# An encoder layer with two mixers: the weave of projection and convolution set to 400:329 instead of 445:329, and eight instead of five steps of the recurrence yielded beside the memory projection

## The chip, the cores and the metric

The kernel runs on one core of a Trainium2 chip. The core has a matrix engine (PE, TensorE), three engines for elementwise work (DVE or VectorE, ACT or ScalarE, POOL or GpSimd), and a queue engine (SP, SyncE) that mostly issues transfers. The metric is the device time of one execution in microseconds; the time of a kernel is the median of its runs.

## The reference, cut to what matters

One layer over 2048 rows of 1024 columns, all in fp32. One projection feeds two mixers: a long convolution (the Hyena half) and a bidirectional recurrence (the mLSTM half). Then come cross-attention into 256 memory rows and an MLP.

```python
u = _rms_norm(h, norm_mix_g[l])
proj = u @ w_in[l]
hy = _short_conv_centred(proj[..., :HY_COLS], hy_conv_w[l], hy_conv_b[l])
y_hy = _group_rms_norm(_hyena(hy, spec, hy_skip[l]), hy_norm_g[l], HYENA_GROUPS)
y_ml = _mlstm_bidirectional(q, k, v, o_pre, gates, ml_gate_b[l])
y_ml = _group_rms_norm(y_ml, ml_norm_g[l], MLSTM_HEADS)
h = h + concat(y_hy, y_ml) @ w_out[l]
h = h + _cross_attention(_rms_norm(h, norm_x_g[l]), _rms_norm(mem, norm_mem_g[l]), wq, wk, wv, wo)
h = h + square(relu(_rms_norm(h, norm_ff_g[l]) @ ff_w1[l])) @ ff_w2[l]
return _rms_norm(h, final_norm_g)
```

The Hyena half applies two filters, one after the other, each by transforms; they are called the first and the second order below. The mLSTM half runs one scan in each direction.

## The kernel before

Each fp32 gemm is split into a high and a low part and done as three products (helper `mm3`: lines 355, 358 and 359). Work is written as generators. Each `yield` carries an estimate of its length, and `weave(a, b, wa, wb)` advances `a` while what it has done, divided by `wa`, is not ahead of what `b` has done, divided by `wb`. So the weights are the lengths in which the two are meant to end together. What is written in this order is then ordered once more, before the run, by a scheduler that simulates the engines; it decides the final order on each engine, and each engine takes its instructions strictly in that order.

The stages that matter here, in the order of the source:

- **Projection and convolution.** `rest` is the projection: `sweep` (transposed columns) and `natural` (rows), with the gates of the recurrence (`gates`) and the states of its backward scan (`states`, fifteen of them, written to `cbd`) at its end. It is woven with `hyena`, the convolution. For each of the two orders the convolution does eight forward transforms (`spectrum`, L173/L186, input `f`; stored to `zs` by POOL's queue), sixteen block steps (L956 for the filter's response, L1030 and L987, loading `zs` and storing `zg`), and eight inverse transforms (L173/L186, input `e`). The first block step of an order needs all eight of its forward transforms.
- **The memory projection.** `memproj` yields eight heads of work: L708 (keys or values from memory), L725 and L737 (folded with the query and output weights). Its weights come through SP's queue (L415).
- **The recurrence.** `mlstm` takes sixteen steps of 128 rows, called chunks here. Chunk n issues the scores of chunk n+1 (L1284), for each direction sixteen products (L1322 within the chunk, L1324 with the state), and the update of the forward state (L1200, then L1206 on DVE). Its row factors are spread by DVE (L1275), masked and scaled by POOL (L1290, L1291), raised by ACT (L1293), multiplied with the scores by DVE (L1294). After every odd chunk the two newest chunks are normalised: squares on ACT (L1349), an inverse square root of thirteen small DVE operations (L211 to L216), then eight scalings (L1356). All products of a chunk go to a ring of four PSUM banks called `hy`, which the convolution and the transposes use too. The first `next` of the generator only loads and issues the scores of chunk 0, so n advances write n-1 chunks.
- **The attention.** It begins with transposes of the mixers' output (L1479) and with w_out, loaded at L1405 and split on ACT and DVE at L366. The remaining chunks are woven into it, and the MLP follows.

`beside_each(n, take(m, 5))` yields one advance of the memory projection and one of the recurrence in turn, with what is left of the five after that.

Of the kernel before, what the change touches and what calls it, by code (L numbers as in the profile page):

```python
# [2076 lines left out]
def chain(*gens):  # L2077
    for g in gens:
        yield from g


def weave(a, b, wa, wb, until=False):
    da = db = 0.0
    fa = fb = False
    while not (fa and fb):
        if fb or (not fa and da / wa <= db / wb):
            try:
                da += next(a)
            except StopIteration:
                fa = True  # L2090
        else:
            try:
                db += next(b)
            except StopIteration:
                fb = True
                if until:
                    return


def program(p):  # L2100
    with ExitStack() as ms:
        with ExitStack() as es:
            p.inproj_open(es)
            p.filters_open()
            p.prepq = p.x_first()
            p.pop()
            s = chain(p.sweep(range(4), 0, True, lambda: p.prep_x(1)), p.opened(), p.sweep(range(4), 1, False))
            f = p.filters()
            for _ in range(5):
                next(s)  # L2110
            next(f)
            next(f)
            next(s)
            weave(s, f, 140, 102, True)
            p.gates_open(es)
            n = p.memproj()
            m = p.mlstm(ms)
            with ExitStack() as hs:
                rest = chain(s, p.sweep(range(4, 10), 1, True), p.natural(1, (3, 0, 1, 2), True),
                             p.natural(0, (3,)), among(p.sweep((4, 5, 8, 9), 0, False), p.gates(), 2),  # L2120
                             among(chain(p.natural(0, (0, 1)), p.sweep((6, 7), 0, False),
                                         p.natural(0, (2,), p.prep_mem, 2)), p.states(), 1),
                             )
                weave(rest, p.hyena(hs), 445, 329)
            for _ in chain(p.turned_in(), take(n, 1), beside_each(n, take(m, 5))):
                pass
        with ExitStack() as rs:
            p.ts = rs.enter_context(ExitStack())
            p.tail_open(p.ts)
            with ExitStack() as at:  # L2130
                g = p.attention(at)
                weave(g, m, 440, 112, True)
                ms.close()
                p.ffn_open(rs)
                for _ in g:
                    pass
            p.ffn()


def among(g, h, every):  # L2140
    for i, v in enumerate(g):
        yield v
        if i % every == every - 1:
            next(h, None)
    for _ in h:
        pass


def beside_each(g, h):
    for v in g:  # L2150
        yield v
        yield next(h, 0)
    yield from h


def take(g, n):
    for _ in range(n):
        v = next(g, None)
        if v is None:
            return  # L2160
        yield v
# [31 lines left out]
```

## Time and profile before

| | us |
|---|---|
| median of 3 runs | 3072.69 |
| lowest and highest run | 3072.32, 3078.89 |
| profiled execution, its own time | 3076.22 |
| span of the profiled execution | 3074.5 |
| PE busy in the span | 2984.5 |
| convolution's last inverse transform (PE) | 1101 |
| chunk 0's scores (PE) | 1115 |
| memory projection's last product ends | 1122 |
| attention's first gemm product | 1179 |

The table's last four rows are times from the start of the span, read from the timeline of PE. In a row of the timeline the first two numbers are the start and the length in microseconds, then come the engine, the source line, the operation, what it writes and reads, its shape, how many instructions were merged, and in square brackets the idle time of that engine before it with what ended it. A matmul's length overlaps with the next one's start, so the pace of PE is read from start to start. Queue rows (SPq, or DMA_DIRECT2D on POOL) show when a transfer is issued.

### The profile page before, as it was taken

The numbers are of one execution on the slowest core, as the hardware profiler recorded it, in microseconds if no ns is written. First come the engines' busy times: TensorE is split into PE (matmuls) and PEld (weight loads), VectorE is DVE, ScalarE is ACT, GpSimd is POOL, SyncE is SP. The second block draws the span as 40 slices with busy tenths as digits, with TensorE's granted clock in tenths as the row PEclk, the third lists the DMA queues.
The fourth block names the chain that finished last, engine by engine and source line by source line (L and its number), as shares of the span: only waits on it lengthen the run. The fifth ranks groups of instructions, "written<-read, shape, count | busy, mean of one in ns | idle before, by whom it ended". The sixth has DMA issues, their size and how long they took to land.

```text
span 3074.5 us, 44129 instructions
## 1 busy us (share of the span) xinstructions
PE 2984.5 (97%) x14799; PEld 2369.8 (77%) x14799; DVE 1938.8 (63%) x3442; ACT 1493.0 (49%) x2930; POOL 1259.7 (41%) x1025
## 2 busy tenths in 40 slices
PE   9999999998999988999999999999999999999998
PEld 7666667775678757888887888888888888888876
DVE  7855454657656347867665665557555676566695
ACT  6443455635654236555544455556555543333335
POOL 0112123411344654333133247765566374344653
PEclk9999999999999988999999999999999999999999
DMA  6655687596877965464567466657544565344434
GB/s 219 196 188 171 214 271 219 184 297 200 258 223 249 349 231 192 158 220 131 188 203 259 147 210 216 208 181 243 186 154 151 195 198 171 118 158 120 155 103 164
DMA packets 423643, 607.03 MB, mean 197 GB/s; under 512 B 36846, under 2 KB 229998, under 8 KB 422392
## 3 DMA queue, kind: packets, MB, share of 16 engines
q1 hardware_dynamic: 395972, 525.42, 53.3%
q0 software_dynamic: 18992, 62.96, 5.6%
q10 hardware_dynamic: 8452, 15.83, 1.4%
q8 instruction: 117, 1.92, 0.3%
q14 instruction: 110, 0.90, 0.1%
HBM read 401.67 MB, written 202.41 MB: 196 GB/s over the span
## 4 chain that ended last, share of the span: by engine, by line
PE 58%; DVE 2%; DMA 1%; issue 1%; ACT 0%; POOL 0%; SPq 0%; DVEq 0%; ACTq 0%; POOLq 0%
PE mm L355 12%; PE mm L359 12%; PE mm L358 12%; PE hy L355 6%; PE hy L359 6%; PE hy L358 6%; PE hy L1322 1%; PE hy L1324 1%; DVE bl L1693 0%; PE hy L1284 0%; PE hy L1479 0%; PE hy L1596 0%; DVE acc L1991 0%; PE hy L1200 0%; DVE acc L2028 0%
## 5 line engine op out<-in xcount | busy, mean ns | idle before, releaser
L1692 ACT CAST ah<-w 128x512 fp32r<-128x512 f32 x284 | 176.7, 623 | 304.0 <-PE hy L358 157.8
L1693 DVE TENSOR_TENSOR bl<-wr,bh 128x512 fp32r<-128x512 f32 x213 | 235.5, 1110 | 131.1 <-ACT bh L1692 131.0
L366 DVE TENSOR_TENSOR wl<-wn,wh 128x512 fp32r<-128x512 f32 (+1 forms) x296 | 216.6, 775 | 94.3 <-ACT wh L366 94.3
L355 PE MATMUL mm<-xh,wh 128*128 128x512 f32 x640 | 263.3, 413 | 3.7 <-ACT wh L366 1.2
L358 PE MATMUL mm<-xl,wh 128*128 128x512 f32 x640 | 254.1, 397 | 4.5 <-DVE xl L366 4.4
L1692 ACT CAST bh<-wr 128x512 fp32r<-128x512 f32 x232 | 143.4, 621 | 229.0 <-PE mm L359 177.5
L359 PE MATMUL mm<-xh,wl 128*128 128x512 f32 x640 | 253.7, 397 | 0.0
L1693 DVE TENSOR_TENSOR al<-w,ah 128x512 fp32r<-128x512 f32 x236 | 213.6, 905 | 55.7 <-ACT ah L1692 55.6
L359 PE MATMUL mm<-bh,al 128*128 128x512 f32 x576 | 223.7, 391 | 4.0 <-DVE al L1693 4.0
L355 PE MATMUL mm<-bh,ah 128*128 128x512 f32 x576 | 225.8, 392 | 0.1
L358 PE MATMUL mm<-bl,ah 128*128 128x512 f32 x576 | 224.9, 390 | 0.0
L366 ACT CAST wh<-wn 128x512 fp32r<-128x512 f32 (+1 forms) x296 | 164.4, 620 | 105.8 <-PE mm L359 51.0
L358 PE MATMUL mm<-act,wh 128*128 128x512 f32 x512 | 202.0, 394 | 0.0
L355 PE MATMUL mm<-act,wh 128*128 128x512 f32 x512 | 199.4, 396 | 2.0 <-ACT wh L366 1.9
L359 PE MATMUL mm<-act,wl 128*128 128x512 f32 x512 | 199.9, 392 | 0.0
L355 PE MATMUL hy<-bh,ah 128*128 128x512 f32 x448 | 175.2, 391 | 0.0
L358 PE MATMUL hy<-bl,ah 128*128 128x512 f32 x448 | 174.6, 390 | 0.0
L359 PE MATMUL hy<-bh,al 128*128 128x512 f32 x448 | 174.4, 390 | 0.0
L331 POOL TENSOR_TENSOR b<-b 128x512 f32<-128x512 f32 x32 | 48.1, 1505 | 294.6 <-DVE b L330 275.2
L355 PEld LDWEIGHTS mm<-xh,wh 128*128 128x128 f32 x640 | 120.5, 188 | 53.1 <-issue 19.4
L358 PEld LDWEIGHTS mm<-xl,wh 128*128 128x128 f32 x640 | 120.6, 188 | 49.2 <-issue 18.6
L355 PE MATMUL mm<-wh,xh 128*128 128x256 f32 (+1 forms) x512 | 154.7, 302 | 0.0
(396 smaller groups left out, 8262.9 us busy)
## 6 DMA issues: line engine op xcount, KB each, us to landing
wr<-hc SPq DMA_DIRECT2D x224, 256.0 KB
w<-in_ff_w_dram SPq DMA_DIRECT2D x172, 256.0 KB
hc<-wn SPq DMA_DIRECT2D x128, 256.0 KB
wn<-in_w_in_dram SPq DMA_DIRECT2D x100, 256.0 KB
hc<-q SPq DMA_DIRECT2D x96, 256.0 KB
fs<-a SPq DMA_DIRECT2D x32, 512.0 KB
zs<-a POOLq DMA_DIRECT2D x32, 512.0 KB, 6.0
a<-fs SPq DMA_DIRECT2D x64, 256.0 KB
```

The costliest lines, as they stand in the source:

```text
L331: nc.gpsimd.tensor_tensor(b, f, b, ALU.subtract)
L355: first = mm(ps, lh, rh, start=start, stop=False)
L358: mm(ps, lh, rl, start=False, stop=False)
L359: self.last = mm(ps, ll, rh, start=False, stop=stop)
L366: both = (self.nc.scalar.copy(hi, src), self.nc.vector.tensor_tensor(lo, src, hi.bitcast(F32), ALU.subtract))
L1322: nc.tensor.matmul(dst, nm[:, h], va[:, h], start=True, stop=state is None)
L1324: nc.tensor.matmul(dst, rows_[d, 1][:, h], state[:, h], start=False, stop=True)
L1692: self.nc.scalar.copy(hi, src)
L1693: eng.tensor_tensor(lo, src, hi.bitcast(F32), ALU.subtract)
```

## The change

Two numbers change. The weight of the projection in the weave goes from 445 to 400, with that of the convolution left at 329: the convolution's turn comes after less projection, and by the source it ends when a tenth of the projection is still to come. And the recurrence is advanced eight times beside the memory projection instead of five: chunks 0 to 6 instead of 0 to 3 are written there, and nine instead of twelve remain to be woven into the attention.

```diff
-                weave(rest, p.hyena(hs), 445, 329)
-            for _ in chain(p.turned_in(), take(n, 1), beside_each(n, take(m, 5))):
+                weave(rest, p.hyena(hs), 400, 329)
+            for _ in chain(p.turned_in(), take(n, 1), beside_each(n, take(m, 8))):
                 pass
```

On PE, from the first scores of the recurrence to the attention's first transposes, the order before is this. L737 is the memory projection's, L1284 are scores, L1200 the state update that ends a chunk (the last of its two rows for each), L1479 a transpose of the attention; between these stand the chunk's L1322 and L1324.

```order
L737 MATMUL mm_10713<-wm_10643,kt_10687 128x512 x2
L1284 MATMUL hy_9927<-qn_9895,kk_t_9896 128x128 x4
L1284 MATMUL hy_10008<-qn_9910,kk_t_9911 128x128 x4
...
L737 MATMUL mm_10731<-wm_10643,kt_10687 128x512 x2
...
L1200 MATMUL hy_10072<-ve_10063,kn_10006 128x129 x2
...
L1200 MATMUL hy_10230<-ve_10220,kn_10159 128x129 x2
...
L1200 MATMUL hy_10415<-ve_10405,kn_10344 128x129 x2
...
L1200 MATMUL hy_10566<-ve_10556,kn_10495 128x129 x2
L1479 MATMUL hy_10776<-ident_60,wn_10766 128x128 x4
```

And with the change:

```order
L1284 MATMUL hy_9927<-qn_9895,kk_t_9896 128x128 x4
L1284 MATMUL hy_10008<-qn_9910,kk_t_9911 128x128 x4
...
L1200 MATMUL hy_10072<-ve_10063,kn_10006 128x129 x2
...
L1200 MATMUL hy_10230<-ve_10220,kn_10159 128x129 x2
...
L737 MATMUL mm_10959<-wm_10643,kt_10789 128x512 x2
...
L1200 MATMUL hy_10415<-ve_10405,kn_10344 128x129 x2
...
L1200 MATMUL hy_10566<-ve_10556,kn_10495 128x129 x2
...
L1200 MATMUL hy_10743<-ve_10733,kn_10672 128x129 x2
...
L1200 MATMUL hy_10888<-ve_10878,kn_10817 128x129 x2
...
L1200 MATMUL hy_11040<-ve_11030,kn_10969 128x129 x2
L1479 MATMUL hy_11108<-ident_60,wn_11098 128x128 x4
```

The memory's last product stood ahead of the updates of chunks 0 to 3, and the transposes behind that of chunk 3; now it stands behind the update of chunk 1, and the transposes behind that of chunk 6, so that five chunks instead of three follow it whole before the attention begins.

On PE at the turn from the first order to the second, before: the last forward transform (input `f1`), then projection and transposes of it, the gates' transpose (L1149), and the first block products (L1030).

```order
L186 MATMUL hy_6867<-a_6639,f1_104 64x512 x2
L831 MATMUL mm_6948<-ident_60,cv_6707 16x128
L355 MATMUL mm_6978<-xh_100,wh_6416 128x512
...
L1149 MATMUL hy_6957<-ident_60,mm_6715 128x1 x2
...
L359 MATMUL mm_6978<-xh_100,wl_6417 128x512
L825 MATMUL mm_7003<-ident_60,cv_6806 128x128 x4
L1030 MATMUL hy_7053<-a_6887,dm_6676 128x512
```

And with the change:

```order
L186 MATMUL hy_6478<-a_6360,f1_104 64x512 x2
L355 MATMUL mm_6552<-xh_100,wh_5876 128x512
...
L359 MATMUL mm_6552<-xh_100,wl_5877 128x512
L956 MATMUL mm_6612<-a_6473,dm_6471 128x512
L956 MATMUL mm_6618<-a_6473,dm_6471 128x512
L1030 MATMUL hy_6625<-a_6498,dm_6397 128x512
```

Twenty-four projection products and two small groups stood between the transform and the block product; now nine projection products and two L956 products stand there.

On SP's queue, the first w_out loads (L1405, tile `we`) stood behind the attention's row loads (L1473), before:

```order
L415 DMA wm_10643<-in_xa_wo_dram 128x1024
...
L1473 DMA wn_10770<-yh_2735 128x512
L1178 DMA kn_10344<-kn_78 128x512
L1473 DMA wn_10772<-yh_2735 128x512
L1405 DMA we_10911<-in_w_out_dram 128x2x256
L1259 DMA kk_t_10428<-kt_77 128x4x128
L1405 DMA we_10915<-in_w_out_dram 128x2x256
```

And with the change:

```order
L415 DMA wm_10305<-in_xa_wv_dram 128x4x256 x2
L1405 DMA we_11269<-in_w_out_dram 128x2x256
L1405 DMA we_11273<-in_w_out_dram 128x2x256
L1405 DMA we_11277<-in_w_out_dram 128x2x256
L415 DMA wm_10444<-in_xa_wo_dram 128x1024 x2
L1405 DMA we_11281<-in_w_out_dram 128x2x256
```

They stood behind the memory's last weights (L415) and now stand among them.

## The prediction

> **What bounds the kernel now.** The page first: the busy line of TensorE (PE) and the two slice lines.
>
> ```profile
> span 3074.5 us, 44129 instructions
> PE 2984.5 (97%) x14799; PEld 2369.8 (77%) x14799; DVE 1938.8 (63%) x3442; ACT 1493.0 (49%) x2930; POOL 1259.7 (41%) x1025
> PE   9999999998999988999999999999999999999998
> PEclk9999999999999988999999999999999999999999
> ```
>
> PE is busy for 2984.5 of 3074.5 us, so 90 us are waits, and the one place where both slice lines show an 8 is slices 14 and 15, about 1078 to 1230 us. The change takes no matmul away and adds none: it can only make the waits and the slow-clock time larger or smaller, and it moves work exactly there. The table of windows for that place, cut at the ends of the state updates (L1200) of the recurrence's steps, called chunks here, is the row on which most of the sum rests. Its columns: window, length, then PE, PEld, DVE, ACT, POOL busy with instruction counts, granted PE clock, DMA share, GB/s.
>
> ```profile
> 1122.20:1126.80 4.60, 3.86 (x32) 3.48 (x30) 2.85 (x11) 2.40 (x10) 3.78 (x6) 1.00 0.73 249
> 1126.80:1138.90 12.10, 7.51 (x48) 7.06 (x48) 6.61 (x22) 8.16 (x34) 7.11 (x6) 0.86 0.95 322
> 1138.90:1159.00 20.10, 11.17 (x49) 10.15 (x50) 14.94 (x55) 9.01 (x36) 9.21 (x10) 0.58 0.39 126
> 1159.00:1166.90 7.90, 7.51 (x49) 7.12 (x47) 5.25 (x17) 4.71 (x22) 3.37 (x3) 0.77 0.48 139
> 1166.90:1179.10 12.20, 6.04 (x33) 5.46 (x33) 8.17 (x30) 8.16 (x28) 3.77 (x4) 0.75 0.55 173
> ```
>
> The memory projection's last product ends at 1122.2; the attention's first gemm product starts at 1179.1. Between them lie the rest of chunk 0, then chunks 1, 2 and 3 with nothing else on PE (12.1, 20.1 and 7.9 us), then the attention's first transposes and the head of chunk 4 (12.2 us): 56.9 us in all. What these instructions need when PE is not waiting is read where chunk 4 stands among gemm products:
>
> ```profile
> 1180.42 0.38 PE L1322 MATMUL hy<-va,rw 128*128 128x129 f32 x2
> 1180.64 0.39 PE L1324 MATMUL hy<-cf,rw 128*128 128x129 f32 x2
> 1150.84 0.64 PE L1322 MATMUL hy<-va,rw 128*128 128x129 f32 x2
> 1151.27 0.64 PE L1324 MATMUL hy<-cbn,rw 128*128 128x129 f32 x2
> ```
>
> From start to start, two take 0.22 us at the full clock (0.11 each) and 0.43 at the slow one. The stretch holds 32+48+49+49+33 = 211 matmuls, 23.2 us of work, so it loses 56.9 - 23.2 = **33.7 us**, the largest single loss in the run. Chunk 2 loses most because of what queues on DVE (VectorE):
>
> ```profile
> 1139.68 2.54 DVE L366 TENSOR_TENSOR wl<-we,wh 128x512 fp32r<-128x512 f32 x3
> 1146.68 0.17 DVE L211 TENSOR_SCALAR hy<-brm 128x8 int32<-128x8 int32 x1 [3.02 <-ACT brm L208]
> 1150.43 2.22 DVE L1356 SCALAR_TENSOR_TENSOR ht<-ht,hy,gml 128x128 f32<-128x128 f32 x8
> 1149.84 0.77 PE L1322 MATMUL hy<-va,rw 128*128 128x129 f32 x2 [2.81 <-DVE bry L213]
> ```
>
> Every second chunk (the even ones, 2, 4, 6) has the normalisation of the two before it in front: DVE waits 3.02 us for the sums, runs 13 small operations from 1146.68 and the L1356 scalings from 1150.43, and only then what the next state update needs. The odd chunk 3 has none of it and takes 7.9 us.
>
> **The change part by part.** *Seven chunks.* In the source, chunks 0 to 6 instead of 0 to 3 are yielded beside the memory projection. What decides is the order of the engines, shown with the change: memory products lie around chunks 0 and 1 only. Chunks 2 to 6 follow the last memory product, and the attention's transposes (L1479) follow chunk 6. PE runs in that order, so **five bare chunks stand where three stood**, three even and two odd.
>
> - An even bare chunk: 20.1 us as measured, less the three weight splits of 2.54 us that DVE ran inside chunk 2. The change puts those splits before the memory ends (the first w_out loads now stand among the memory's loads on SP's queue). 20.1 - 2.5 = 17.6 us. Bounds: 12.1 (chunk 1, bare and without the normalisation) and 20.1. I take 17.6, since DVE's rows in chunk 2 stand in the same order after the change.
> - An odd one: 7.9 us (bounds 7.9 and 12.1).
> - Chunk 2 starts when chunk 1's update is done, and three L737 products of the memory still cover its start. In the trace such a product is two instructions, and 16 of them take 7.03 us (row below): 6 x 0.44 = 2.65 us come off.
> - The tail from chunk 6 to the first gemm: 12.2 us now, with 5.17 us of waiting for the splits of the transposed rows. The 13 normalisation operations (about 0.21 us each, 2.7 in all) ran among these splits on DVE; after chunk 6 none is due. 9.5 us (bounds 7 and 12.2).
>
> ```profile
> 1091.48 7.03 PE L737 MATMUL mm<-wm,kt 128*128 128x512 f32 x16
> 1174.90 1.12 PE L1479 MATMUL hy<-ident,wn 128*128 128x128 f32 x4 [5.17 <-DVE act L366]
> 1173.57 0.17 DVE L213 COPY bry<-hy 128x8 f32<-128x8 f32 x1
> 1173.77 0.17 DVE L214 TENSOR_TENSOR hy<-hy,bry 128x8 f32<-128x8 f32 x1
> ```
>
> The new stretch: 3 x 17.6 + 2 x 7.9 - 2.65 + 9.5 = 75.45 us. It holds 5 x 49 + 33 = 278 matmuls, 30.6 us, and so loses 44.9 us instead of 33.7: **+11.2 us**. Counting loss and not length settles what moved: chunk 1 under the memory and three chunks out of the attention take their matmul time with them, and all of it is PE time either way.
>
> *What covers the rest.* Chunks 0 and 1 now run among 18 products of L737 and 16 of L708; if that cover fails, chunk 1 costs its bare loss of 12.1 - 5.3 = 6.8 us. Against it stand two waits of the memory stage that more neighbours may fill, 2.31 and 2.94 us. I take 0 (bounds -5.3 and +6.8). The attention loses three of its twelve chunks. With them PE is busy for 20.00 us in each of the four windows of 20 us from 1200 to 1280 (first and last below), so their leaving gives nothing there; the longest wait for a chunk's DVE work behind that is 1.38 us (bounds -1.4 and 0).
>
> ```profile
> 1011.66 3.03 PE L725 MATMUL mm<-kt,wm 128*128 128x256 f32 x8 [2.31 <-ACT kt L710]
> 1086.33 1.16 PE L1200 MATMUL hy<-va,kn 128*128 128x129 f32 x8 [2.94 <-POOL va L1196]
> 1200.00:1220.00 20.00, 20.00 (x101) 16.96 (x101) 17.02 (x35) 14.80 (x40) 11.12 (x8) 1.00 0.56 173
> 1260.00:1280.00 20.00, 20.00 (x114) 17.40 (x113) 14.64 (x44) 12.26 (x43) 6.42 (x5) 1.00 0.42 132
> 1298.77 0.66 PE L1596 MATMUL hy<-ident,e 128*128 128x128 f32 x4 [1.38 <-DVE cf L1206]
> ```
>
> *The convolution ahead.* At 400 instead of 445 the convolution gets its turn in the weave after about a tenth less projection. Its sixteen block steps of the second order shrink from 778 to 562 numbered rows of PE's order, and its last inverse transforms leave the memory stage in part (three beside it, not six). Projection covers each step; where it is thinner is the turn from the first order to the second:
>
> ```profile
> 700.17 0.39 PE L355 MATMUL mm<-xh,wh 128*128 128x512 f32 x1
> 700.40 0.39 PE L358 MATMUL mm<-xl,wh 128*128 128x512 f32 x1
> 728.88 0.63 PE L186 MATMUL hy<-a,f 32*64 32x512 f32 x7
> 731.04 1.05 POOL L339 DMA_DIRECT2D zs<-a  x2 [2.47 <-ACT st L201]
> 736.26 1.16 SPq L920 DMA_DIRECT2D a<-zs  x2
> 739.70 3.49 PE L1030 MATMUL hy<-a,dm 128*128 128x512 f32 x4 [3.62 <-DMA a<-zs]
> 743.58 1.88 PE L956 MATMUL mm<-a,dm 128*128 128x512 f32 x4
> ```
>
> The last forward transform ends at 729.5; its result is stored by POOL's queue, loaded by SP's, and multiplied at 739.7: 10.2 us, of which 6.6 are filled and 3.62 waited. In the changed order nine projection products (0.23 us from start to start, 2.1) and two L956 rows (1.9) fill 4.0, so 6.2 are waited: **+2.6 us** (bounds 0 and +6.6). Two other waits nearby trade places: the scan of the gates gets more cover, and an inverse, a forward and an inverse transform come with no projection between.
>
> ```profile
> 705.97 0.64 PE L173 MATMUL hy<-a,f 32*64 32x512 f32 x1 [1.30 <-DVE a L1051]
> 712.62 0.37 PE L1134 MATMUL hy<-ident,ends 128*1 128x128 f32 x1 [2.70 <-DVE ends L1129]
> 714.81 1.03 PE L173 MATMUL hy<-a,e 64*32 64x512 f32 x1 [1.81 <-issue]
> ```
>
> The 2.70 may go and two like 1.30 and 1.81 come: 0 (bounds -4.5 and +3.1).
>
> **Sum:** +11.2 + 2.6 = +13.8 us on the profiled execution, 3076.22 to 3090.0. That execution stands 3.5 us above the median of the runs, 3072.69; on the median the sum is **3086.5 us**.
>
> [...] Chunk 1 has the one long wait, for a load that came late to ACT:
>
> ```profile
> 1135.22 0.67 PE L1322 MATMUL hy<-va,rw 128*128 128x129 f32 x2 [4.58 <-DVE den L1330]
> 1131.78 1.28 ACT L1194 ACTIVATE ve<-va,cols 128x129 f32<-128x129 f32 x4 [3.94 <-DMA va<-vd]
> ```
>
> In chunk 2 the granted clock was 0.58, though no wait of PE there exceeded 2.81 us. [...]
>
> **The rivals.** *The clock stays whole.* The bare chunks get no wait as long as the one in chunk 1 and run at the full clock. For: that 4.58 us wait came with a late load of chunk 1, which now lies under the memory. Against: 0.58 and 0.77 in two chunks running. An even chunk has 49 matmuls at 0.215 instead of 0.11, 5.1 us less, 12.5 us: 37.5 + 15.8 - 2.65 + 9.5 - 30.6 - 33.7 + 2.6 = -1.6, or 3071 us, no change.
>
> *Faster: the chunks pipeline.* With no attention work between them, every bare chunk keeps chunk 3's pace of 7.9 us because the normalisation, on DVE and ACT, slips into time that PE spends on the next one. Place: between the memory's end and the first gemm. Price: 5 x 7.9 - 2.65 + 9.5 - 30.6 - 33.7 + 2.6 = -15.4, 3057 us. It decides from an even chunk under 13.0 us (3E + 15.8 - 2.65 + 9.5 - 30.6 + 2.6 = 33.7), and passes 0.2% under 11. Against: DVE is in order and its normalisation rows stand ahead of what the update waits for.
>
> *Slower still: the weave starves.* The denser convolution waits for stores and loads at several places; with the upper bounds of its two terms (+6.6, +3.1) and an even chunk of 20.1: 13.8 + 4.0 + 3.1 + 7.5 = +28, 3101 us.
>
> **How the numbers follow.** 0.2% (6.1 us) is about what a measurement of this kernel can tell from no change. The forecast has 0.55, the starving weave 0.10, the whole clock 0.20, the pipelining chunks 0.15. So slower 0.65, same 0.20, faster 0.15. The likeliest case alone spans 3078 to 3098. The range for 8 in 10 takes in the whole clock and the starving weave, and leaves out the pipelining chunks: 3068 to 3102.
>
> **What would show it.** Right: after the last L737, five L1200 updates before the first L1479, even ones about 17 us apart from the one before and odd ones about 8, a granted clock near 0.6 there, and an L1030 wait near 6 us on a zs load. Wrong: even chunks under 13 us, a clock near 1.0 in them, or new PE waits among the memory products or in the weave that sum to over 6 us.

## The result and the profile after

The changed kernel takes 3111.36 us in the median (3107.58 to 3116.31) against 3072.51 us, a ratio of **1.0123 (95% interval 1.0103 to 1.0144)**: 38.8 us slower. The forecast was 3086.5 us and its range ended at 3102. The direction was right; the size was 2.8 times what was forecast.

The page of the changed kernel first: span, busy time, and the slice lines of PE and its granted clock.

```profile
span 3105.9 us, 44184 instructions
PE 2994.5 (96%) x14799; PEld 2372.8 (76%) x14799; DVE 1944.3 (63%) x3442; ACT 1493.1 (48%) x2930; POOL 1262.3 (41%) x1025
PE   9999999988999996999999999999999999999998
PEclk9999999999999997999999999999999999999999
```

PE waits 111.4 us (3105.9 - 2994.5) instead of 90, and its busy time has grown by 10 us with the same matmuls: that is slow clock (over the span the mean granted clock is 0.984 instead of 0.987). The profiled executions stand 31.4 us apart (3107.58 and 3076.22); the one of after is the fastest of its four runs, the one of before lies above its median, so what follows explains 31 of the 39 us. The slices have two dents now. The one at slice 15 was expected. The 8s at slices 8 and 9 (621 to 776 us), where the kernel before shows a 9 and an 8, were not: they lie in the weave of projection and convolution.

The expected dent, by windows cut at the ends of the state updates (columns as in the prediction):

```profile
1161.98:1176.35 14.37, 7.99 (x50) 7.33 (x49) 10.16 (x42) 6.17 (x26) 7.84 (x9) 0.72 0.74 259
1176.35:1183.51 7.16, 6.79 (x49) 6.41 (x47) 5.24 (x17) 4.67 (x22) 3.70 (x4) 0.85 0.55 154
1183.51:1201.36 17.85, 9.23 (x49) 8.48 (x50) 12.27 (x51) 8.44 (x36) 9.84 (x10) 0.74 0.43 145
1201.36:1207.98 6.62, 6.25 (x48) 5.87 (x47) 5.24 (x17) 4.67 (x22) 3.60 (x4) 0.92 0.56 163
1207.98:1225.88 17.90, 9.24 (x50) 8.48 (x50) 12.28 (x51) 8.45 (x36) 9.88 (x10) 0.73 0.45 147
1225.88:1231.40 5.52, 5.46 (x32) 5.27 (x31) 2.84 (x6) 4.99 (x17) 0.92 (x1) 0.65 0.68 209
```

Five bare chunks and the tail to the first gemm: 14.4, 7.2, 17.9, 6.6, 17.9 and 5.5 us, 69.4 in all. With 30.6 us of matmuls that loses 38.8 us instead of 33.7. In the last window PE is busy for 5.46 of 5.52 us: the wait of 5.17 us that the tail held before is gone whole.

The weave, by windows from 339 us to the memory projection's first product. Before: the first order's forward transforms, the turn (its inverse and the second order's forward transforms), the second order's block steps, and the whole.

```profile
339.00:424.00 85.00, 80.66 (x463) 56.66 (x462) 41.10 (x63) 41.46 (x64) 9.97 (x17) 1.00 0.81 280
611.60:739.70 128.10, 115.36 (x779) 83.37 (x778) 83.80 (x221) 50.07 (x88) 20.31 (x30) 0.97 0.80 262
739.70:935.40 195.70, 193.51 (x904) 136.51 (x905) 124.05 (x200) 123.06 (x213) 77.59 (x83) 0.99 0.73 224
339.00:988.10 649.10, 624.80 (x3472) 456.58 (x3471) 386.42 (x710) 354.27 (x606) 194.70 (x224) 0.99 0.75 238
```

The same four of the changed kernel:

```profile
339.00:417.00 78.00, 67.69 (x379) 44.84 (x380) 31.46 (x49) 33.35 (x52) 9.95 (x17) 0.93 0.83 284
600.50:722.50 122.00, 105.76 (x791) 78.07 (x789) 60.79 (x107) 42.66 (x77) 18.56 (x29) 0.94 0.85 265
722.50:909.60 187.10, 173.97 (x657) 111.37 (x658) 142.53 (x288) 125.16 (x212) 64.24 (x66) 0.96 0.68 204
339.00:1023.20 684.20, 638.23 (x3492) 460.24 (x3493) 405.84 (x759) 355.38 (x609) 206.26 (x238) 0.97 0.75 232
```

Length less PE's busy time is waiting: 24.3 us before, 46.0 after, so 21.7 more. By an estimate from the last rows, the clock of 0.97 instead of 0.99 costs another 0.03 x 684 - 0.01 x 649 = 14 us. Together **36 us, in a place where the prediction had 2.6**.

For the experiments a finer count is used. The *lost time* of a stretch is its length less what its matmuls take at the pace that the split gemms and the recurrence keep in the trace of before where nothing stops them, from start to start (0.23 us for 512 columns, 0.13 for 272, 0.12 for 256, 0.11 for 128 and 129). The products of the block steps and of the memory projection count at that pace too, though they take nearly twice as long at a clock of 1.00 (28 of L725, 256 columns, 6.15 us from start to start; 16 of L737, 512 columns, 7.03). Pieces of transforms, many of them side by side (eight of 512 columns in 0.69 us), count as nothing. So only differences between kernels mean something. Stages: the weave (339 us to the memory's first product), the memory (to its last), and behind the memory (to the attention's first gemm product).

| lost us | weave | memory | behind it | rest | sum |
|---|---|---|---|---|---|
| before | 134.7 | 61.9 | 36.7 | | |
| after | 171.6 | 56.3 | 40.4 | | |
| difference | +36.9 | -5.6 | +3.7 | -5.1 | +29.9 |

The sum falls 1.5 us short of the 31.4 between the two executions. A few us of the weave's plus and the memory's minus are three inverse transforms that moved from the one to the other. Kernels whose PE order is the same up to the memory lost 170.2 to 177.3 (after and three below) or 134.7 and 137.0 us in the weave, so a difference under some 7 us is within what executions of one order differ by, and a smaller one below is a hint at most.

### The profile page after: what moved, and what is told of

The parts are those of the page before. It is cut to its first block, busy times and chain, and to the rows that moved or that the text cites. A ratio compares the mean times of both kernels' runs of the same rounds, so it can differ in the third digit from the quotient of the medians.

```text
span 3105.9 us, 44184 instructions
## 1 busy us (share of the span) xinstructions
PE 2994.5 (96%) x14799; PEld 2372.8 (76%) x14799; DVE 1944.3 (63%) x3442; ACT 1493.1 (48%) x2930; POOL 1262.3 (41%) x1025
## 3 DMA queue, kind: packets, MB, share of 16 engines
q1 hardware_dynamic: 395972, 525.42, 53.3%
## 4 chain that ended last, share of the span: by engine, by line
PE 78%; DMA 7%; DVE 6%; issue 5%; ACT 2%; POOL 1%; SPq 1%; DVEq 0%; POOLq 0%; ACTq 0%
PE mm L355 16%; PE mm L358 16%; PE mm L359 16%; PE hy L359 6%; PE hy L355 6%; PE hy L358 6%; PE hy L173 2%; PE mm L956 1%; PE hy L1030 1%; PE hy L987 1%; DMA va<-vd 1%; PE hy L1322 1%; PE hy L1200 1%; PE hy L1324 1%; PE mm L737 1%
## 5 line engine op out<-in xcount | busy, mean ns | idle before, releaser
L1522 POOL TENSOR_TENSOR ssum<-ssum,sq 128x512 f32<-128x512 f32 x56 | 80.3, 1435 | 195.5 <-ACT sq L1521 187.2
```

What stands on the lines that cost most here:

```text
L1522: nc.gpsimd.tensor_tensor(ssum, ssum, sq, ALU.add)
```

## The experiments

All ratios are against runs of before on the same chip, whose median was 3071.3 to 3074.9 us; the column us is the run's own median. The three columns of lost time are read from one execution each.

| run | weight, steps, and what else | us | ratio (95% interval) | weave | memory | behind |
|---|---|---|---|---|---|---|
| w400t5 | 400, 5 | 3093.0 | 1.0055 (1.0040 to 1.0069) | 170.2 | 55.3 | 21.5 |
| w445t8 | 445, 8 | 3092.4 | 1.0054 (1.0039 to 1.0069) | 137.0 | 59.5 | 56.0 |
| w422t5 | 422, 5 | 3074.4 | 0.9998 (0.9987 to 1.0008) | 143.1 | 61.9 | 27.7 |
| w470t5 | 470, 5 | 3078.2 | 1.0011 (1.0001 to 1.0020) | 134.1 | 63.3 | 39.3 |
| w385t5 | 385, 5 | 3073.8 | 1.0003 (0.9992 to 1.0013) | 164.1 | 52.2 | 12.9 |
| gates_late | 400, 5, gates later | 3090.3 | 1.0058 (1.0043 to 1.0073) | 170.4 | 57.9 | 21.9 |
| dense_first | 445, 5, first transforms dense | 3071.0 | 0.9991 (0.9980 to 1.0003) | 142.5 | 55.3 | 34.3 |
| dense_turn | 445, 5, turn dense | 3071.5 | 0.9993 (0.9982 to 1.0004) | 143.3 | 68.6 | 21.1 |
| dense_blocks2 | 445, 5, second blocks dense | 3070.6 | 0.9987 (0.9977 to 0.9996) | 141.5 | 64.4 | 22.8 |
| dense_first_blocks2 | 445, 5, both | 3073.6 | 1.0003 (0.9992 to 1.0013) | 144.5 | 59.8 | 27.2 |
| undo_turn | 400, 5, turn as before | 3098.1 | 1.0085 (1.0072 to 1.0099) | 163.6 | 57.8 | 26.8 |
| undo_blocks2 | 400, 5, second blocks as before | 3095.8 | 1.0085 (1.0072 to 1.0098) | 172.8 | 56.8 | 26.9 |
| undo_first | 400, 5, first transforms as before | 3068.2 | 0.9987 (0.9979 to 0.9995) | 150.1 | 55.0 | 25.9 |
| head_only | 400, 5, only its later start | 3086.9 | 1.0043 (1.0026 to 1.0060) | 159.3 | 59.4 | 25.1 |
| spectra_only | 400, 5, only its transforms' pace | 3077.4 | 1.0015 (1.0004 to 1.0027) | 163.2 | 53.3 | 21.1 |
| after_norm_sbuf | after, inverse root in SBUF | 3118.2 | 1.0145 (1.0131 to 1.0159) | 176.7 | 58.9 | 44.4 |
| after_norm_sbuf_ht4 | and four buffers of ht | 3104.4 | 1.0095 (1.0081 to 1.0109) | 177.3 | 53.2 | 35.7 |
| undo_first_ht4 | undo_first with both | 3077.9 | 1.0006 (0.9996 to 1.0016) | 151.3 | 51.9 | 19.3 |

### The two halves of the change, and other weights

```diff
-                weave(rest, p.hyena(hs), 400, 329)
+                weave(rest, p.hyena(hs), 445, 329)        # w445t8; w422t5 has 422, w470t5 has 470
-            ... beside_each(n, take(m, 8))):
+            ... beside_each(n, take(m, 5))):              # w400t5, w422t5, w470t5
```

> Only the weight of the weave is changed (400), five steps beside the memory as before. In the profiled runs of before and after, the convolution's stretch loses about 30 us more (idle and slow clock) and the bare stretch of chunks about 5 more. Theory A, thin cover in the weave: the 30 us are here too; two bare chunks instead of three behind the memory give about 14 us back, so 3088 us (3080 to 3098). Theory B, the cost comes from the seven chunks beside the memory: the weave's loss is an accident of where the later stages start, and this kernel stays at 3058 to 3078 us.

> Only the steps beside the memory are changed (eight), the weave's weight is that of before. By the order seven updates follow the memory's last product instead of four. Theory A: the weave loses what it lost before (idle between 340 and 988 us within 2 us of before's), chunks 4, 5 and 6 come bare with losses of about 12.5, 1.5 and 12.5 us, less some 8 us from a shorter tail and the attention: about +19 us, 3091 us (3084 to 3098). Theory B: 3100 to 3112 us.

> The weight halfway (422), five steps. By the order three updates follow the memory's last product instead of four. Theory A, dose and effect: about half the weave's extra loss (12 to 18 us), 5 to 8 us back behind the memory, 3080 us (3074 to 3088). Rival C, chance: the scheduler's order lines waits up in a new way at any other weight, so 422 costs as much as 400 or more (3090 to 3105 us).

> The weight on the other side (470), five steps: more projection between the convolution's steps. Theory A: the weave's loss shrinks by 5 to 15 us, part of it given back because the convolution ends later, 3064 us (3056 to 3073). Rival C, chance: 445 stands in a lucky spot and any other weight costs, 3085 to 3100 us.

Each half alone costs about the same, 0.55%, and the two make 1.1% of the 1.23%: they add up. Theory B (the steps beside the memory explain all) fell with both. The weight alone moves +35.5 us into the weave and takes 15 back behind the memory, because chunks 0 and 1 get done among the memory's products. The eight steps alone leave the weave as it was and add 19.3 us behind the memory. Their chunks 4, 5 and 6 are what the prediction priced; the windows of w445t8:

```profile
1166.00:1183.83 17.83, 8.88 (x49) 8.12 (x50) 12.25 (x51) 8.42 (x36) 10.19 (x11) 0.75 0.44 146
1183.83:1190.65 6.82, 6.46 (x49) 6.07 (x47) 5.24 (x17) 4.68 (x22) 3.60 (x4) 0.89 0.56 159
1190.65:1209.01 18.36, 9.24 (x49) 8.48 (x50) 13.22 (x51) 8.53 (x36) 9.70 (x10) 0.73 0.44 143
```

The weave's loss by weight is no straight line: 134.1 at 470, 134.7 at 445, 143.1 at 422, 170.2 at 400. More projection between the steps (470) gains nothing, against theory A; most of the cost sets in between 422 and 400, and at 422 the second order's block steps alone already hold 11.8 us of waits, against 2.2 before. Theory C (any other weight costs as much) fell too.

### One piece at a time

In gates_late the gates (L1076 on) move into the next stretch of the projection; the other runs lower what a piece of the convolution announces, at weight 445, so that this piece alone gets a tenth less projection.

```diff
+ gates_late:    ... p.sweep((4, 5, 8, 9), 0, False), ... chain(p.gates(), p.states()), 1),
+ dense_blocks2: yield 4.6 if o == 0 else 4.14     (was 4.6)
+ dense_turn:    yield 4.5 if o else 5.4           (was 6.0)
+ dense_first:   yield 46.8 ... yield 3.78         (was 52, 4.2)
```

The wait that led to gates_late, PE and then DVE in the changed kernel:

```profile
776.42 2.04 PE L956 MATMUL mm<-a,dm 128*128 128x512 f32 x2 [7.12 <-DVE a L960]
```

```profile
771.15 0.28 DVE L1114 TENSOR_TENSOR pad<-pad 64x128 f32<-64x128 f32 x1
771.46 0.29 DVE L1115 TENSOR_TENSOR pad<-pad 64x128 f32<-64x128 f32 x1
...
773.86 0.15 DVE L1129 COPY ends<-pad 64x1 f32<-64x1 f32 x1
774.04 0.69 DVE L1034 TENSOR_TENSOR b<-hy,a 128x512 f32<-128x512 f32 x1
774.77 0.69 DVE L959 COPY a<-mm 64x512 f32<-64x512 f32 x1
775.47 0.69 DVE L960 COPY a<-mm 64x512 f32<-64x512 f32 x1
```

DVE runs the scan of the gates, one small step after the other (with one copy of the projection, L782, of 1.07 us among them), and only behind it L1034 and the copies L959 and L960 that free the PSUM banks of the block step. PE stands still for 7.12 us. Before, the same scan ran at 700 to 712 us, among transforms, where it cost waits of 1.30 and 2.70.

> Weight 400 and five steps, but the gates of the recurrence are written with the backward states, later: by the order their transposes now stand behind the last block product of the second order instead of between two of its block steps. In the run with weight 400 and five steps the second order's block steps lost 56.7 us (41.1 before) and held one wait of 7.11 us for DVE's L960. Theory A1, thin cover alone: the block steps still lose 52 to 58 us. Theory A2, the gates' scan on DVE stands in the way: that wait is gone and they lose 42 to 48 us. The whole: the states come later too, so one more bare chunk or states among the memory products may give it back; 3080 us (3072 to 3092).

> Weight 445 and five steps; only the second order's sixteen block steps announce a tenth less (4.14 instead of 4.6), so that they alone get a tenth less projection between them. The gates stay where they were before, ahead of these steps. Theory A1: their loss rises by 12 to 16 us over before's 41.1. Theory A2: by less than 6 us. Behind the memory three updates follow instead of four, which gives back about 9 us: 3078 us by A1, 3066 us by A2.

> Weight 445 and five steps; only the first order's inverse transforms with the second order's forward transforms announce a tenth less (5.4 instead of 6.0). By the order the gates then stand among the second order's block steps, as with weight 400, though these steps are as dense as before. Theory A1: the turn loses about 10 us more (30.9 before), the block steps nothing more. Theory A2: the block steps lose 8 to 14 us more. Two updates instead of four follow the memory's last product, about 15 us back: 3068 us by A1 alone, 3068 by A2 alone, 3078 by both.

> Weight 445 and five steps; only the first order's forward transforms announce a tenth less (3.78 instead of 4.2, and 46.8 instead of 52 for the head). Theory A1: the stretch of these transforms loses 7 to 10 us more (16.6 before), the later ones nothing; four updates follow the memory's last product as before: 3081 us. Rival: the dense start is a place where the order happened to line up badly at 400, and nothing is lost (3070 to 3075 us).

In gates_late the 7.11 us wait is gone and the block steps lose 50.5 instead of 56.7 us: the scan is worth about 6 us of the 36 there, between what theories A1 and A2 had. It buys nothing in all. The weave as a whole loses as much as without the edit (170.4 and 170.2); of that, the part ahead of the block steps, whose order on PE is the same in both kernels, came out 5.4 us longer in this execution (385.0 and 379.6). In the memory stage a wait for L710 grows from 2.44 to 5.29 us. dense_blocks2 costs 4.9 us in its own piece, dense_first 7.2; dense_turn costs nothing in the turn (29.9 against 30.9) and 7.4 in the block steps, among which the gates' last transposes (L1149) now stand; the scan itself is done ahead of them. Each piece gets its cost back or more behind the memory, in the memory or both. Alone, no piece makes the kernel slower, so the 3081 us that A1 gave for dense_first, and the 3078 us for dense_blocks2, did not come; the weave's pluses add to 23 us (7.8 + 8.6 + 6.8), not 36.

dense_turn also shows where a gain goes: it saves 15.6 us behind the memory and loses 6.7 in it, in one wait.

```profile
1060.16 5.51 PE L725 MATMUL mm<-kt,wm 128*128 128x256 f32 x16 [9.09 <-ACT o L715]
```

### One piece undone at weight 400

```diff
+ undo_turn:    yield 4.5 if o else 6.675          (was 6.0)
+ undo_blocks2: yield 4.6 if o == 0 else 5.1175    (was 4.6)
+ undo_first:   yield 57.85 ... yield 4.6725       (was 52, 4.2)
```

> Weight 400 and five steps, with the turn (first order's inverse and second order's forward transforms) at the density of before (6.675 announced instead of 6.0). With weight 400 and five steps the weave between 339 us and the memory's first product lost 170.2 us, the turn in it 41.5 (before: 134.7 and 30.9). If the pieces add up: the turn back to 31, the rest unchanged, the weave loses about 160, three updates behind the memory instead of two take 6 us back: 3088 us. Rival, the pieces multiply (each dense piece is cheap alone, dear when what stands ahead of it is dense too): later pieces fall as well, the weave loses under 152: 3078 us or less.

> Weight 400 and five steps, with the second order's block steps at the density of before. They lost 56.7 us at weight 400 and 41.1 before; alone dense they lost 46.0. The gates still stand among them. If the pieces add up: 5 us less and the gates' part stays, the weave loses 165 us, three updates behind the memory: 3093 us. If they multiply: the block steps fall to 47 or less, the weave below 160, 3085 us or less.

> Weight 400 and five steps, with the first order's forward transforms at the density of before. That stretch lost 23.9 us at weight 400, 16.6 before. If the pieces add up: the weave loses 163 us, three updates behind the memory: 3092 us. If they multiply (a dense start pulls all that follows into thinner cover): the turn or the second block steps fall too, the weave below 155: 3082 us or less.

undo_turn takes 7 us from the weave, all of it in the turn (34.0 against 41.5), and undo_blocks2 nothing; both are slower than weight 400 alone (1.0085 against 1.0055), slower than either theory had them. The profiled execution of undo_turn lies 10.5 us below its median, so its lost time does not show where that comes from. undo_first takes 20 us and is the only one below before. Its first transforms lose 22.2 us, hardly less than the 23.9 at weight 400; the gain is in what follows, the turn (36.2 against 41.5) and above all the second block steps (45.6 against 56.7), whose announced lengths it doesn't touch. That looks as if the pieces multiplied, but it is not shown: the edit also moved more of the projection among those block steps. The third window of after above has 657 matmuls on PE; the same steps in undo_first, and then in undo_turn, have

```profile
721.20:912.60 191.40, 184.63 (x809) 124.98 (x810) 142.75 (x284) 126.80 (x219) 66.22 (x73) 0.99 0.70 214
718.40:920.90 202.50, 188.71 (x792) 127.33 (x793) 141.54 (x289) 128.13 (x218) 69.57 (x72) 0.96 0.64 197
```

DVE has the same work in undo_first as in after (284 and 288 instructions, 142.75 and 142.53 us), but PE waits 6.8 us instead of 13.1, and the clock is 0.99 instead of 0.96. More matmuls around the steps are not the reason: undo_turn has nearly as many and waits 13.8 us.

### Density or phase

Two readings are left: how much projection stands between the convolution's steps (density), or which part of the projection they meet (phase).

```diff
+ head_only:           yield 57.85                 (was 52; weight 400)
+ spectra_only:        yield 4.6725                (was 4.2; weight 400)
+ w385t5:              weave(rest, p.hyena(hs), 385, 329)
+ dense_first_blocks2: dense_first and dense_blocks2 together
```

> Weight 400 and five steps; of the two edits of the run that undid the first transforms only one: the convolution's first turn comes later (57.85 announced instead of 52), its transforms are as dense as at weight 400. That run lost 150.1 us in the weave, the one with nothing undone 170.2. Density theory (how much projection stands between the steps decides): 163 to 172 us, 3086 to 3094 us in all. Phase theory (which part of the projection the steps meet decides): 148 to 156, 3066 to 3076 us.

> The other half of it: at weight 400 and five steps the first order's forward transforms announce 4.6725 instead of 4.2, so that they are as dense as before, and the convolution begins where it begins at weight 400. Density theory: the weave loses 148 to 156 us, 3064 to 3074 us in all (two bare updates fewer). Phase theory: 163 to 172 us, 3085 to 3094 us.

> Weight 385 and five steps, denser still. By the order one update follows the memory's last product. Density theory, the loss grows with the density (before 134.7, at 422 143.1, at 400 170.2): 178 to 195 us in the weave, about 8 us back behind the memory: 3094 to 3112 us. Phase theory: no trend, 140 to 165 us, 3055 to 3080 us.

> Weight 445 and five steps, with both the first order's forward transforms and the second order's block steps a tenth denser; each alone ran about 4 us below before. Adding up: the weave loses 149 us, the memory 57, three updates follow it: 3068 us. Multiplying: the second block steps lose 52 or more and it is slower than before, 3078 us or more.

Neither reading is alone in it. The two edits of undo_first take 11 and 7 us in the weave, about what they take together (20), but 7 is at the limit of what is read here, and by whole time only spectra_only (1.0015) is clear of weight 400 alone (1.0055); head_only (1.0043) is not. Neither run met one theory's forecast in both its loss and its time. At 385 the weave loses 164.1 us, no more than at 400, which speaks against density alone; yet every kernel at weight 400 or below lies between 150 and 177, whatever its shift, and every one at 422 or more between 134 and 145, which speaks against phase alone. dense_first_blocks2, with two dense pieces at 445, loses 144.5 us in the weave, less than adding up gave (149), and its second block steps wait 5.3 us with no more matmuls around them than undo_turn has:

```profile
732.00:915.70 183.70, 178.43 (x797) 122.86 (x798) 122.14 (x240) 119.23 (x208) 70.07 (x76) 0.97 0.71 215
```

So two dense pieces do not multiply there. One thing sorts the kernels better than the weight: where DVE's scan of the gates (its first L1114) starts, seen from the second order's first block product (L1030).

| the scan starts | kernels | waits of PE in the second block steps | lost in the weave |
|---|---|---|---|
| 23 to 68 us ahead of it | before, w470t5, the four dense runs | 2.2 to 6.9 us | 134 to 145 us |
| 4 us ahead of it | w422t5, undo_first | 11.8 and 6.8 us | 143.1 and 150.1 us |
| 17 to 52 us behind it | after, w400t5, w385t5, undo_turn, undo_blocks2, head_only, spectra_only | 10.7 to 14.3 us | 159 to 173 us |
| behind all sixteen steps | gates_late | 7.5 us | 170.4 us |

The last row keeps this from being shown as the cause: with the scan out of the block steps their waits fall, but the weave's loss does not. At 385 the kernel is as fast as before: the memory and the place behind it give back 33.5 us (9.7 and 23.8) against the 29.4 that the weave lost. **What tips the weave between 422 and 400 stays open**; that it is there, and that no single wait carries it, is shown.

### The even chunk

The prediction laid its 17.6 us to the normalisation's rows on DVE. The inverse root (L211 to L216) works in a bank of the PSUM ring; here it works in SBUF, and then ht, too, gets two more buffers.

```diff
-                rv = self.bank_rsqrt(sb, ss, 128)
+                nm_ = sb.tile([128, 8], F32, tag="brm", name="brm", bufs=2)
+                nc.scalar.activation(nm_, ss, AF.Identity, bias=self.eps, scale=1.0 / 128)
+                rv = self.rsqrt(sb, nm_, "nr")
-                    y = sb.tile([128, 4, 128], F32, tag="h0", name="ht", bufs=2)
+                    y = sb.tile([128, 4, 128], F32, tag="h0", name="ht", bufs=4)   # ht4 runs
```

> The changed kernel, with one thing else: the inverse square root of the recurrence's normalisation works in SBUF and takes no bank of the ring of four PSUM banks. In the changed kernel the even bare chunks took 14 to 18 us and hold waits of 2.1 to 5.0 us of L1322 for DVE's L213, L215 or L1356. Theory D, the bank is what PE waits for: these waits shrink to what DVE's queue leaves, the three even chunks come to about 13 us each, the whole 8 to 14 us faster than the changed kernel: 3100 us. Rival, DVE's order is what PE waits for: the normalisation stands ahead of the row that PE needs anyway, the chunks stay at 16 to 18 us: 3108 to 3114 us.

> The changed kernel with the inverse square root in SBUF and, further, four buffers of the output tile ht instead of two. With two, PE's wait of 10.3 us in each even bare chunk was for ACT's L1336, and that waited 5.45 us for the store of ht to finish. Theory E, the two buffers of ht close the even chunk's chain (squares, inverse root, scalings, store, next output): the wait falls to 3 to 5 us, even chunks from 18.3 to about 12 us, 18 us less than with the SBUF root alone: 3098 us (3091 to 3106). Rival, DVE's in-order queue sets it (its thirteen or ten small operations stand ahead of the rows the chunk needs): even chunks stay at 16 to 18 us, 3110 us or more.

> The same two edits of the normalisation on the run with weight 400, five steps and the first transforms undone (3068.2 us, 0.9987 of before), which has one even bare chunk. Theory E: one even chunk 5 to 8 us shorter, 3062 us, 0.997 of before. Rival: no change, 3068 us.

Taking the bank away gained nothing: after_norm_sbuf is no faster than the changed kernel (1.0145 against 1.0123, with intervals that overlap), and its bare chunks 4 and 6 take 18.4 and 18.3 us. One long wait took the place of another. In chunk 4 of the changed kernel PE waits most for the root's bank (L213), and little for L1336, which there waits for no store:

```profile
1192.20 0.77 PE L1322 MATMUL hy<-va,rw 128*128 128x129 f32 x2 [4.98 <-DVE bry L213]
1199.27 2.09 PE L1200 MATMUL hy<-ve,kn 128*128 128x129 f32 x8 [2.12 <-ACT ht L1336]
```

In chunk 4 of after_norm_sbuf, one row each of PE, ACT, DVE and POOL:

```profile
1209.27 2.09 PE L1200 MATMUL hy<-ve,kn 128*128 128x129 f32 x8 [10.31 <-ACT ht L1336]
```

```profile
1208.59 1.14 ACT L1336 ACTIVATE ht<-hy,den 128x128 f32<-128x128 f32 x4 [5.45 <-DMA ym<-ht]
```

```profile
1204.51 2.19 DVE L1356 SCALAR_TENSOR_TENSOR ht<-ht,nr_y,gml 128x128 f32<-128x128 f32 x8
```

```profile
1206.18 0.58 POOL L1358 DMA_DIRECT2D ym<-ht  x1 [3.13 <-DVE ht L1356]
```

Read backwards: PE waits for ACT's L1336, which reads the finished product out of PSUM into ht. ACT waits for the store of the old ht, the store for DVE's scalings, these for the inverse root. There are two buffers of ht and the normalisation holds both until they are stored. With four, the even chunks fall to 11.6, 8.5 and 10.9 us, as theory E had it, but the odd ones grow (chunk 3 and 4 of after_norm_sbuf_ht4 here), because the normalisation has slipped into them:

```profile
1174.29:1187.86 13.57, 8.21 (x50) 8.01 (x49) 11.64 (x37) 6.56 (x28) 8.04 (x8) 0.75 0.48 156
1187.86:1196.36 8.50, 7.38 (x49) 7.00 (x47) 7.09 (x24) 4.97 (x23) 3.04 (x3) 0.80 0.50 150
```

Behind the memory 8.7 us less are lost than with the root alone (35.7 against 44.4) and 4.7 less than in the changed kernel; theory E had 18 us for the whole. Four buffers with the root left in its bank were not run, so what the buffers are worth alone stays open. On undo_first the same two edits save 6.6 us there, and the attention takes more than that back (1.0006 against 0.9987): its transposes wait for rows that are stored later.

```profile
1193.44 1.09 PE L1479 MATMUL hy<-ident,wn 128*128 128x128 f32 x4 [9.31 <-DMA wn<-ym]
```

Nothing beat before by much: undo_first and dense_blocks2 are both at 0.9987, about 4 us, and the upper ends of their intervals (0.9995, 0.9996) only just leave out no change, in two of eighteen runs.

## Why the prediction was wrong

- **The chunks: right in their lengths, in part by luck.** Forecast: five bare chunks in place of three, 17.6 us an even one, 7.9 an odd one, a stretch that loses 11.2 us more. Measured: 17.9 and 17.9 (14.4 for the covered one, 14.95 forecast), 7.2 and 6.6; the loss grew by 5.1. The tail was over-sized, 9.5 against 5.5 us: all of its wait went, not only the 2.7 us of the normalisation. The luck is in the even chunk: 2.5 us of waiting were taken off the 20.1 for the weight splits, but by the windows the waits fell only from 8.9 us (20.10 - 11.17) to 8.6 (17.85 - 9.23); the rest is PE's own time, 11.17 against 9.23 us, at a clock of 0.74 instead of 0.58. Taken apart, the stretch is +19.3 from the eight steps and some -15 from the weight.
- **The cause of an even chunk: half right.** DVE's normalisation does delay it, in the changed kernel through the bank of its root (4.98 us). But its place in DVE's queue is not all: with the bank out of the way the chunk is as long, because the two buffers of ht tie the next output to the last store (5.45 us of ACT's wait).
- **The memory stage: at its lower bound.** 0 was taken, with bounds -5.3 and +6.8; -5.6 by the count above, with the transforms that left it. What is left of the kernel, the attention in it, gave 5.1 us, where 0 was taken for the attention.
- **The weave: here it failed.** The step reads "Projection covers each step; where it is thinner is the turn from the first order to the second", at +2.6 us with bounds 0 and +6.6, from one wait in one place. That place came out as forecast: 6.2 us of waiting, and the L956 and L1030 at its end waited 1.66 and 4.29 us, 5.95 in all, against 3.62 before. The weave lost some 34 us more elsewhere, which the step left out as covered: in many waits (four of them in the rows below, ahead of the two of the forecast place, and the 7.12 us above) and in a granted clock of 0.97 instead of 0.99.

```profile
347.50 0.64 PE L173 MATMUL hy<-z,f 32*64 32x512 f32 x1 [2.69 <-ACT a L311]
380.02 1.08 PE L173 MATMUL hy<-a,f 32*64 32x512 f32 x1 [3.90 <-DMA a<-hy]
393.10 0.80 PE L173 MATMUL hy<-a,f 32*64 32x512 f32 x1 [3.70 <-ACT a L998]
626.92 1.06 PE L173 MATMUL hy<-a,e 64*32 64x512 f32 x1 [3.41 <-DMA a<-zg]
717.15 1.12 PE L956 MATMUL mm<-a,dm 128*128 128x512 f32 x2 [1.66 <-ACT P L788]
722.56 2.90 PE L1030 MATMUL hy<-a,dm 128*128 128x512 f32 x3 [4.29 <-DMA a<-zs]
```

- **A sentence of that step was wrong in sign.** "The scan of the gates gets more cover": it fell among the second order's block steps instead and held DVE for the 7.12 us wait; moving it away was worth some 6 us there and nothing in the weave as a whole.
- **The rivals.** The starving weave was the case that came nearest, at 0.10 and with 28 us for the whole, but not as it was priced: 7.5 of the 28 stood for even chunks of 20.1 us, which did not come, and its two bounds in the weave, 6.6 and 3.1, are those of two places, while the loss was spread over many. The clock did not stay whole (0.72 to 0.74 in even chunks). That it does where no wait is as long as chunk 1's 4.58 us was the author's assumption, which no run shows: chunks 4 and 6 of the changed kernel hold waits of 4.98 and 5.03 us, but its chunk 2 holds none over 2.16 us and had a clock of 0.72. And no even chunk came under 13 us in the changed kernel.

The bounds of the weave's term were the error behind the range: they (0 and +6.6, and -4.5 and +3.1 for the two waits nearby) came from single waits that could be seen in the run before, while the term stood for 650 us in which the order of PE was new throughout.

## What to carry to other kernels

A weight that shifts two interwoven streams is not priced at its thinnest place: compare the whole stretch's waiting and granted clock, and take a range as wide as the waits that hundreds of re-ordered rows can form. What one edit gives at one stage and takes at the next is seen only in a ledger of lost time by stage; here -24 behind the memory stood against +29 in the weave at one weight and made no difference at all. When a wait is taken away and another of the same length appears, follow the chain to the next buffer: here first the bank of the root, then the two output tiles.

## What the runs showed of the hardware that was not expected

The clock fell with no long wait ahead of it. In the turn of the changed kernel, PE's rows between 689 and 698 us, and the window behind them:

```profile
689.71 0.61 PE L173 MATMUL hy<-a,e 64*32 64x512 f32 x1
692.18 0.64 PE L173 MATMUL hy<-a,f 32*64 32x512 f32 x1 [1.39 <-DVE a L1051]
694.55 1.06 PE L173 MATMUL hy<-a,e 64*32 64x512 f32 x1 [1.02 <-ACT a L998]
697.82 2.93 PE L956 MATMUL mm<-a,dm 128*128 128x512 f32 x3 [1.31 <-DMA a<-fs]
```

```profile
695.00:700.00 5.00, 3.69 (x19) 1.10 (x4) 1.29 (x2) 0.00 (x0) 0.84 (x2) 0.50 1.01 322
```

From 675 to 690 us PE is busy all the time, at a clock of 1.00. Then the waits are 1.0 to 1.4 us, with the small pieces of transforms (32 x 64 and 64 x 32) between them; the granted clock is 0.50, and a group that took 0.61 us (first row) takes 1.06 (third row). In the kernel before, the clock was 0.64 from 1134.0 to 1138.8 us, a stretch that begins in the long wait of chunk 1; in chunk 2 it was back at 1.00 and fell again, without such pieces:

```profile
1138.80:1142.10 3.30, 1.25 (x9) 0.97 (x8) 3.30 (x7) 3.30 (x11) 1.67 (x2) 1.00 0.70 215
1142.20:1162.60 20.40, 13.61 (x58) 12.78 (x59) 13.53 (x53) 8.16 (x38) 8.57 (x8) 0.50 0.35 110
```

Ahead of this fall PE is busy for 1.25 of 3.30 us, with products of 128 x 128, and no wait in the two windows is over 2.81 us. What makes the clock fall is not shown by these runs. Its price comes on top of the waits: by the estimate above, about 14 of the weave's 36 us are slow clock.
